# Attention scores in a hybrid decoder block: the lo rows of the queries copied to both partition halves

## The chip, the cores and the metric

The kernel runs on one core of a Trainium2 chip. The metric is the device time of one execution in microseconds, median over the runs. Names of engines: PE is TensorE (PEld its weight loads), DVE is VectorE, ACT is ScalarE, SP is the queue that issues most DMAs; ACT's queue issues some as well.

## The reference, cut to what matters

One layer (DEPTH is 1) over a sequence of 2048 tokens, width 1024, float32. A pre-norm and one combined input projection feed three mixers: a Mamba-2 style SSD with 16 heads, a Conformer convolution with 31 taps, and sliding-window attention with 8 query heads, 2 key-value heads of 64 channels, window 128 and blocks of 128 queries. Their outputs go through one output projection, a post-norm with residual, and a gated per-layer embedding. The attention scores, which the change touches, are

```
s = jnp.einsum('bnqkgd,bnskd->bnkgqs', q, kb).astype(jnp.float32) * (ATTN_HEAD_DIM ** -0.5)
...
s = jnp.where(valid[None, :, None, None], s + bias, -jnp.inf)
m = jnp.maximum(jnp.max(s, axis=-1, keepdims=True), sink)
e = jnp.exp(s - m)
probs = e / (jnp.sum(e, axis=-1, keepdims=True) + jnp.exp(sink - m))
```

For a block of 128 queries `kb` holds 256 keys: the block before and the block itself.

## The kernel before, in words

**Numbers.** Most products run in TensorE's float32r form. Each operand is split into hi (the rounded value) and lo (the rest, exactly), and a product is the sum of hi x lo, lo x hi and hi x hi: three matmuls in `proj` (L443 to L445), `mm3` (L207 to L209) and the output projection (L1042 to L1044).

**Stages.** Phase 1 makes the mixers' outputs and writes them to DRAM; phase 2 is the output projection, phase 3 the gated embedding. Tokens go in four chunks of 512; phase 1 handles them in two halves of two chunks. In each half a list of units is worked through (`C`, `A`, `S`, `G`: convolution, attention, SSD, second B/C group), each for the two chunks p = 0 and p = 1. `A0` to `A3` are the attention units: unit `Aj` does heads j and j + 4, one from each key-value group, in one 128-column projection tile.

**Order.** A unit has a front (a generator that issues projections and evictions and yields every four or eight steps) and a back (softmax and so on), put on the list `pending`. `drive` runs a front; at each yield it advances every pending back by one step and issues some of the waiting convolution taps (L691 on DVE, three per yield in `A` units). The program order so made goes through a scheduler that assigns buffers and orders the instructions of each engine at compile time; on the chip every engine then works its own queue in order.

**Attention.** `attn_front` projects the queries (24 matmuls), evicts them as hi on ACT (`qh`, L708) and lo on DVE (`ql`, L709), copies, and projects the gate (another 24). The keys of a chunk lie ready in two tiles `kT[c][0]` and `kT[c][1]`, one for each key-value group: in partitions 64\*hh to 64\*hh + 63 the hi rows of group hh, in the other 64 partitions its lo rows. So that one matmul over 128 rows gives hi x hi and hi x lo, the hi rows of a query head are needed in both halves: four DMAs on ACT's queue (L713) copy the 64 rows of head hh from `qh` into both halves of `qq[hh]`. The third product, lo x hi, is a second matmul over the 64 rows of `ql` and of the keys where the hi rows lie.

`attn_back` has steps: `scores(0)`, `softmax(0)`; `scores(1)`, `softmax(1)`; `turn(0)`; `mix(0)`, `turn(1)`; `mix(1)`. `scores(u)` fills two PSUM banks (tag `m`, two in all, one for each head) for query blocks 2u and 2u + 1: for each head and block one output of 256 columns, or, for the first block of a chunk, two of 128 columns (the keys before the chunk come from another tile; in the very first block they are left out). DVE (L764) adds the bias, writes the scores to SBUF with their maximum and so frees the banks. ACT takes the exponentials (L790), DVE normalises (L799), PE transposes (L810), ACT copies the transposes out (L817), PE multiplies them with the values (L832).

For p = 0 the steps of the back run between the projections of p = 1; for p = 1 between those of the next unit.

Of the kernel before, what the change touches and what calls it, by code (L numbers as in the profile page):

```python
# [14 lines left out]
P = 128  # L15
# [46 lines left out]
def hybrid_block_kernel(  # L62
# [31 lines left out]
    def t512(name, dtype=F32):  # L94
        return wk.tile([P, TC], dtype, tag="t", name=name, bufs=10)
# [7 lines left out]
    def act_tiles():  # L103
        """(hi, lo) float32r tiles for two 128-channel tiles of one chunk"""
        return act.tile([P, 2, TC], F32R, tag="ah", name="ah"), act.tile([P, 2, TC], F32R, tag="al", name="al")

# [31 lines left out]
    def rsqrt_cols(dst, src, mul, add):  # L138
        """dst = (src * mul + add) ** -0.5 for a few columns, by Newton's iteration."""
        n = src.shape[1]  # L140
        v = wk.tile([P, n], F32, tag="rs_v", name="rs_v", bufs=2)
        V.tensor_scalar(out=v, in0=src, scalar1=mul, scalar2=add, op0=ALU.mult, op1=ALU.add)
        gi = wk.tile([P, n], I32, tag="rs_i", name="rs_i", bufs=2)
        V.tensor_scalar(out=gi, in0=v.bitcast(I32), scalar1=1, scalar2=None, op0=ALU.arith_shift_right)
        g = wk.tile([P, n], F32, tag="rs_g", name="rs_g", bufs=2)
        V.tensor_scalar(out=g.bitcast(I32), in0=gi, scalar1=-1.0, scalar2=float(0x5F3759DF), op0=ALU.mult, op1=ALU.add)
        t = wk.tile([P, n], F32, tag="rs_t", name="rs_t", bufs=2)
        for it in range(3):
            V.tensor_tensor(out=t, in0=g, in1=g, op=ALU.mult)
            V.scalar_tensor_tensor(out=t, in0=t, scalar=-0.5, in1=v, op0=ALU.mult, op1=ALU.mult)  # L150
            V.scalar_tensor_tensor(out=(dst if it == 2 else g), in0=t, scalar=1.5, in1=g, op0=ALU.add, op1=ALU.mult)

    def col_sums(*ts):
        """PSUM [P, n * NB]: sums over the partitions of each t [P, TC], tokens on partitions"""
        pst = ps("m")
        for i, t in enumerate(ts):
            for b in range(NB):
                o_ = 2 * (i * NB + b)
                PE.matmul(pst[:, o_:o_ + 2], lhsT=t[:, b * P:(b + 1) * P], rhs=ones[:, 0:2], start=True, stop=True)
        return pst[:, 0:2 * NB * len(ts)].rearrange("p (b two) -> p b two", two=2)[:, :, 0]  # L160
# [4 lines left out]
    def rstd_cols(ssum, mul, add):  # L165
        """(sums over partitions * mul + add) ** -0.5, tokens on partitions"""
        r = cols()
        rsqrt_cols(r, col_sums(ssum), mul, add)
        return r

    def make_row(r):
        """the column values of r [P, n * NB] as n rows of TC tokens in DRAM"""
        n = r.shape[1]
        pt = ps("m")
        PE.transpose(pt[0:n, 0:P], r, ident)
        rt = wk.tile([n, P], F32, tag="rt", name="rt", bufs=2)
        A.copy(rt, pt[0:n, 0:P])
        row = dram.tile([n // NB, TC], F32, tag=f"row{n}", name="row", bufs=12 if n == NB else NCHUNK)
        nc.scalar.dma_start(out=row.rearrange("i (b t) -> (i b) t", t=P), in_=rt)
        return [row[i, :] for i in range(n // NB)]  # L180

    def load_row(row, rb_=None):
        """[P, TC] tile with a row on every partition"""
        if rb_ is None:
            rb_ = t512("rb_")
        nc.sync.dma_start(out=rb_, in_=row.partition_broadcast(P))
        return rb_
# [5 lines left out]
    def load_w(src, nk=KD):  # L193
        """src [P, nk, P] -> (hi, lo) float32r tiles with hi + lo == src exactly."""
        st = wp.tile([P, KD, P], F32, tag="wst", name="wst", bufs=2)
        nc.sync.dma_start(out=st[:, 0:nk, :], in_=src)
        hi = wp.tile([P, KD, P], F32R, tag="whi", name="whi", bufs=5)
        lo = wp.tile([P, KD, P], F32R, tag="wlo", name="wlo", bufs=5)
        split(hi[:, 0:nk, :], lo[:, 0:nk, :], st[:, 0:nk, :])
        return hi, lo  # L200

    def mm3(out, w, acts, nk, start=True, stop=True):
        """out += sum_k w[:, k].T @ act_k, each as hi*hi + hi*lo + lo*hi."""
        hi, lo = w
        for k in range(nk):
            ah, al = acts(k)
            PE.matmul(out, lhsT=hi[:, k, :], rhs=al, start=start and k == 0, stop=False)  # L207
            PE.matmul(out, lhsT=lo[:, k, :], rhs=ah, start=False, stop=False)  # L208
            PE.matmul(out, lhsT=hi[:, k, :], rhs=ah, start=False, stop=stop and k == nk - 1)  # L209

    # Work is emitted as a stream of projection steps; the mixers' own stages of earlier
    # pieces are slotted between the steps.
# [7 lines left out]
    def sumsq(tiles):  # L220
        """sum of squares of pair tiles over all their channel tiles"""
# [19 lines left out]
    def put(dst, i, src, late=False):  # L241
        """operands i and i + 1 of a chunk from a pair tile"""
# [10 lines left out]
    def stats(c):  # L253
        """rows of the norms that precede the output projection"""
# [30 lines left out]
    def prep(c, ys):  # L285
        """operands of the output projection for chunk c, in the order in which it takes them"""
# [56 lines left out]
    # =====================================================================  # L343
    # Phase 1: pre-norm, input projection and the three mixers
    # =====================================================================
    with ExitStack() as c1:
# [38 lines left out]
        # The first chunk is projected from the weighted input, the projections being scaled by  # L385
        # the norm afterwards, until its norm is there.
        def add_weighed(c, x_, i):
            """operands from two channel tiles scaled by the pre-norm weight alone"""
# [36 lines left out]
        def pre_apply(c):  # L425
            """normalised operands of chunk c"""
# [10 lines left out]
        def proj(ws, c):  # L437
            """project chunk c with each weight tile of ws; yields between steps, returns PSUM tiles"""
# [14 lines left out]
        def dt_tile():  # L453
            """(hi, hi beside lo) of the step-size columns: their two products share a pass"""
# [25 lines left out]
        def ssd_conv(pj, ci, rs_=None):  # L480
            """causal 4-tap convolution and SiLU of one 128-channel tile."""
# [13 lines left out]
        def silu2(pj, name):  # L495
            """2 * silu of a projection in PSUM."""
# [207 lines left out]

        def attn_front(j, p, c, bias, wq, wg):
# [4 lines left out]
            qq = [t512("qq", F32R), t512("qq", F32R)]  # L710
            for hh in range(2):
                for o_ in range(2):
                    nc.scalar.dma_start(out=qq[hh][64 * o_:64 * o_ + 64, :].bitcast(F32), in_=qh[64 * hh:64 * hh + 64, :].bitcast(F32))  # L713
# [3 lines left out]
            pending.append(attn_back(j, c, bias, qq, ql, g2))  # L717
            yield

        def prev(c, i):  # L720
            """the last block of the chunk before c: keys of the two groups, or values"""
# [11 lines left out]
        def attn_back(j, c, bias, qq, ql, g2):  # L733
# [8 lines left out]
            def scores(u):  # L742
# [3 lines left out]
                for hh in range(2):  # L746
                    for bb in range(2):
                        b = 2 * u + bb
                        r = slice(64 * hh, 64 * hh + 64)
# [8 lines left out]
                        for out, kk in parts:  # L758
                            PE.matmul(out, lhsT=qq[hh][:, qs], rhs=kk, start=True, stop=False)  # L759
                            PE.matmul(out, lhsT=ql[r, qs], rhs=kk[r, :], start=False, stop=True)  # L760
# [110 lines left out]
        def ssd_back(q, p, c, Ab, xv, z2, tiles, tabs):  # L871
# [19 lines left out]
            # decayed C and decay matrices  # L891
# [8 lines left out]
            # chunk states  # L900
# [115 lines left out]
    # =====================================================================  # L1016
    # Phase 2: output projection, post-norm and residual
    # =====================================================================
    with ExitStack() as c2:
# [4 lines left out]
        for c in range(NCHUNK):  # L1024
# [3 lines left out]
            # two column pairs side by side at first: the later operands may come later  # L1028
# [39 lines left out]
        # =================================================================  # L1068
        # Phase 3: gated per-layer embedding
        # =================================================================  # L1070
# [22 lines left out]
def _bucket_onehot(np):  # L1093
    """Row b of the result marks the offsets of bucket b, the last row those out of the window."""
# [104 lines left out]
```

## Time and profile before

| what | value |
|---|---|
| runs | 1899.07, 1901.77, 1907.16 us, median 1901.77 |
| profiled execution | span 1898.5 us from first to last instruction, 25052 instructions; 0.6 us below the fastest run |
| mean granted TensorE clock | 0.991 |
| PE busy | 1865.7 us, 98% |
| DVE busy | 1388.0 us, 73% |
| ACT busy | 821.3 us, 43% |
| first and last score matmul | 131.1 and 1241.1 us after the span's start |
| copies of the queries | 64 DMAs of 128 KB on ACT's queue |

How to read it: a row of the timeline has start, duration, engine, line, operation, output <- inputs and shape. Matmuls are pipelined and their ends are modelled, so what a matmul costs in a stream is the distance from its start to the next one's start. The views of waits tell which engine stood idle before an instruction and what ended that.

### The profile page before, as it was taken

How to read it: one execution, taken by the hardware profiler on the slowest of the kernel's cores; microseconds unless marked ns; L12 is line 12 of the kernel's file. 1: busy time of each engine (PE TensorE's matmuls, PEld its weight loads, DVE VectorE, ACT ScalarE, POOL GpSimd, SP SyncE). 2: the span in 40 equal slices, each digit the busy share in tenths (PEclk: the TensorE clock that was granted, in tenths of full speed). 3: DMA queues.
4: the chain of work that ended last, by engine and by line, in shares of the span. 5: the costliest groups of instructions: out<-in, count | busy, mean ns of one | idle time of the engine just before them, and what ended most of it. 6: DMA issues, size and time to landing. Idle time of an engine off the chain costs nothing.

```text
span 1898.5 us, 25052 instructions
## 1 busy us (share of the span) xinstructions
PE 1865.7 (98%) x9386; PEld 1484.6 (78%) x9386; DVE 1388.0 (73%) x2400; ACT 821.3 (43%) x1565; POOL 0.2 (0%) x4
## 2 busy tenths in 40 slices
PE   7999999999999999999999999999999999999999
PEld 5867777787787778778778777777888878887887
DVE  6868678758868875886885886988787767556543
ACT  5435325423825542461553253264553534443332
POOL 0000000000000000000000000000000000000000
PEclk9999999999999999999999999999999999999999
DMA  7432223222532433132232232225677766678553
GB/s 242 123 119 86 67 79 92 65 82 62 161 106 70 133 115 90 43 107 80 78 125 76 57 100 73 83 91 193 234 240 244 235 227 202 209 233 280 187 193 127
DMA packets 113862, 256.69 MB, mean 135 GB/s; under 512 B 11595, under 2 KB 19404, under 8 KB 113740
## 3 DMA queue, kind: packets, MB, share of 16 engines
q1 hardware_dynamic: 108428, 246.65, 40.3%
q10 hardware_dynamic: 5312, 8.44, 1.9%
q8 instruction: 74, 1.21, 0.3%
q14 instruction: 48, 0.39, 0.1%
HBM read 205.05 MB, written 39.50 MB: 129 GB/s over the span
## 4 chain that ended last, share of the span: by engine, by line
PE 80%; DMA 7%; DVE 6%; ACT 4%; issue 2%; SPq 0%; ACTq 0%; DVEq 0%
PE ps_pp L443 15%; PE ps_pp L444 15%; PE ps_pp L445 15%; PE ps_pp L1042 4%; PE ps_pp L1043 4%; PE ps_pp L1044 4%; PE ps_pp L208 3%; PE ps_pp L209 3%; PE ps_pp L207 3%; PE ps_m L760 2%; PE ps_m L759 2%; PE ps_y L934 2%; PE ps_y L832 2%; PE ps_y L931 1%; DMA Ab<-acs_d 1%
## 5 line engine op out<-in xcount | busy, mean ns | idle before, releaser
L443 PE MATMUL ps_pp<-al,whi 128*128 128x512 f32 x1344 | 539.3, 402 | 11.9 <-DVE al L393 9.7
L445 PE MATMUL ps_pp<-ah,whi 128*128 128x512 f32 x1344 | 536.7, 399 | 0.0
L444 PE MATMUL ps_pp<-ah,wlo 128*128 128x512 f32 x1344 | 536.5, 399 | 0.0
L191 DVE TENSOR_TENSOR wlo<-wst,whi 128x1024 fp32r<-128x1024 f32 x214 | 234.2, 1101 | 172.0 <-ACT whi L190 171.4
L443 PEld LDWEIGHTS ps_pp<-al,whi 128*128 128x128 f32 x1344 | 254.9, 190 | 74.0 <-issue 10.1
L190 ACT CAST whi<-wst 128x1024 fp32r<-128x1024 f32 x214 | 203.0, 951 | 251.4 <-PE ps_pp L445 70.8
L691 DVE SCALAR_TENSOR_TENSOR acc<-gl,par_sb,acc 128x1024 f32<-128x1024 f32 x240 | 307.3, 1281 | 2.4
L445 PEld LDWEIGHTS ps_pp<-ah,whi 128*128 128x128 f32 x1344 | 254.9, 190 | 58.4 <-issue 7.3
L444 PEld LDWEIGHTS ps_pp<-ah,wlo 128*128 128x128 f32 x1344 | 255.0, 190 | 56.9 <-issue 5.0
L489 DVE SCALAR_TENSOR_TENSOR cv<-raw,par_sb,cv 128x512 f32<-128x512 f32 x144 | 107.5, 747 | 24.1 <-ACT cv L487 23.4
L208 PE MATMUL ps_pp<-ah,wlo 128*128 128x512 f32 x256 | 100.8, 394 | 4.1 <-DVE wlo L191 4.1
L1042 PE MATMUL ps_pp<-bl,whi 128*128 128x512 f32 x256 | 101.4, 398 | 0.6 <-ACT whi L190 0.6
L1042 PE MATMUL ps_pp<-al,whi 128*128 128x512 f32 x256 | 100.5, 393 | 0.8 <-DVE al L191 0.8
L1043 PE MATMUL ps_pp<-bh,wlo 128*128 128x512 f32 x256 | 100.9, 394 | 0.0
L207 PE MATMUL ps_pp<-al,whi 128*128 128x512 f32 x256 | 100.4, 392 | 0.3 <-ACT whi L190 0.3
L1044 PE MATMUL ps_pp<-bh,whi 128*128 128x512 f32 x256 | 100.7, 394 | 0.0
L209 PE MATMUL ps_pp<-ah,whi 128*128 128x512 f32 x256 | 100.3, 392 | 0.0
L1043 PE MATMUL ps_pp<-ah,wlo 128*128 128x512 f32 x256 | 100.0, 391 | 0.1
L1044 PE MATMUL ps_pp<-ah,whi 128*128 128x512 f32 x256 | 100.0, 391 | 0.0
L790 ACT ACTIVATE S<-S,nm 128x256 f32<-128x256 f32 (+1 forms) x128 | 62.8, 494 | 58.6 <-DVE nm L776 58.6
L897 ACT ACTIVATE Ab<-Ab,acs 128x128 f32<-128x128 f32 x256 | 82.7, 391 | 0.4
L764 DVE CUSTOM_DVE_ANT_0 S<-ps_m,bias,par_sb 128x256 f32<-128x256 f32 (+1 forms) x128 | 58.9, 467 | 5.4 <-PE ps_m L760 5.4
(235 smaller groups left out, 2624.2 us busy)
## 6 DMA issues: line engine op xcount, KB each, us to landing
wst<-in_w_in_dram SPq DMA_DIRECT2D x88, 512.0 KB, 3.5
wst<-in_w_out_dram SPq DMA_DIRECT2D x64, 512.0 KB, 4.3
Ab<-acs_d SPq DMA_DIRECT2D x64, 256.0 KB, 4.0
ysd<-y_d SPq DMA_DIRECT2D x32, 512.0 KB, 5.9
wst<-in_w_gate_dram SPq DMA_DIRECT2D x32, 512.0 KB, 3.5
gl<-in_xT_dram SPq DMA_DIRECT2D x16, 512.0 KB, 3.7
qq<-qh ACTq DMA_DIRECT2D x64, 128.0 KB, 3.0
y_d<-cv SPq DMA_DIRECT2D x32, 256.0 KB, 3.3
```

Source lines behind the costliest of these rows:

```text
L190: A.copy(hi, src)
L191: V.tensor_tensor(out=lo, in0=src, in1=hi.bitcast(F32), op=ALU.subtract)
L207: PE.matmul(out, lhsT=hi[:, k, :], rhs=al, start=start and k == 0, stop=False)
L208: PE.matmul(out, lhsT=lo[:, k, :], rhs=ah, start=False, stop=False)
L209: PE.matmul(out, lhsT=hi[:, k, :], rhs=ah, start=False, stop=stop and k == nk - 1)
L443: PE.matmul(o_, lhsT=hi[:, k, :], rhs=al, start=k == 0, stop=False)
L444: PE.matmul(o_, lhsT=lo[:, k, :], rhs=ah, start=False, stop=False)
L445: PE.matmul(o_, lhsT=hi[:, k, :], rhs=ah, start=False, stop=k == KD - 1)
L691: V.scalar_tensor_tensor(out=acc, in0=gl[:, k:k + 2 * TC], scalar=pc("ccw", j * 31 + k), in1=acc, op0=ALU.mult, op1=ALU.add)
L1042: PE.matmul(pj[dd], lhsT=hi[:, i, :], rhs=yl, start=first, stop=False)
L1043: PE.matmul(pj[dd], lhsT=lo[:, i, :], rhs=yh, start=False, stop=False)
L1044: PE.matmul(pj[dd], lhsT=hi[:, i, :], rhs=yh, start=False, stop=last)
```

## The change

Beside `qh` the lo rows are copied to both partition halves as well. Both go to tiles of one shape, [128 partitions, 2 heads, 512 tokens], from a new ring of three buffers (tag `qd`); `qh` and `ql` stay in the common ring of ten 512-column tiles. Eight DMAs in place of four are issued on ACT's queue in each attention unit. Both score matmuls then take all 128 rows of the key tile: the second one computes lo x hi and lo x lo, where it computed lo x hi before. The number of matmuls stays.

```
+        def qpair(name):
+            return tp.tile([P, 2, TC], F32R, tag="qd", name=name, bufs=3)
+
         def attn_front(j, p, c, bias, wq, wg):
...
-            qq = [t512("qq", F32R), t512("qq", F32R)]
-            for hh in range(2):
-                for o_ in range(2):
-                    nc.scalar.dma_start(out=qq[hh][64 * o_:64 * o_ + 64, :].bitcast(F32), in_=qh[64 * hh:64 * hh + 64, :].bitcast(F32))
+            qq = [qpair("qh2"), qpair("ql2")]
+            for o_ in range(2):
+                r = slice(64 * o_, 64 * o_ + 64)
+                for t, src in zip(qq, (qh, ql)):
+                    for hh in range(2):
+                        nc.scalar.dma_start(out=t[r, hh, :].bitcast(F32), in_=src[64 * hh:64 * hh + 64, :].bitcast(F32))
...
-            pending.append(attn_back(j, c, bias, qq, ql, g2))
+            pending.append(attn_back(j, c, bias, qq, g2))
...
-                        r = slice(64 * hh, 64 * hh + 64)
...
-                            PE.matmul(out, lhsT=qq[hh][:, qs], rhs=kk, start=True, stop=False)
-                            PE.matmul(out, lhsT=ql[r, qs], rhs=kk[r, :], start=False, stop=True)
+                            for i, t in enumerate(qq):
+                                PE.matmul(out, lhsT=t[:, hh, qs], rhs=kk, start=i == 0, stop=i == 1)
...
-    nc = _bacc.Bacc("TRN2", target_bir_lowering=False, num_devices=1)
+    nc = _bacc.Bacc("TRN2", target_bir_lowering=False, num_devices=1, dynamic_dma_scratch_size=1024)
```

The last line makes a reserved scratch area in SBUF smaller, which leaves room for the new ring; the kernel issues no DMA from GpSimd. The rest of the diff takes out comments and docstrings, by which line numbers move.

More of the change, by code (lines that the diff above doesn't have):

```diff
@@ L731, in keep_tail, with attn_back @@
                 kv_tail.append(t)
-        def attn_back(j, c, bias, qq, ql, g2):
+        def attn_back(j, c, bias, qq, g2):
             S, mx, den, nm = {}, {}, {}, {}
```

## The prediction

> **What bounds the kernel now.** I read the page first, its busy shares and its chain of waits.
>
> ```profile
> PE 1865.7 (98%) x9386; PEld 1484.6 (78%) x9386; DVE 1388.0 (73%) x2400; ACT 821.3 (43%) x1565; POOL 0.2 (0%) x4
> ...
> PE 80%; DMA 7%; DVE 6%; ACT 4%; issue 2%; SPq 0%; ACTq 0%; DVEq 0%
> ```
>
> TensorE (PE) is busy all the time and the chain runs through it for 80%. A microsecond taken out of PE's stream is therefore a microsecond of the kernel, as long as PE does not then wait for somebody else. How much the score matmuls take is not to be read from their durations, whose ends are modelled and overlap, but from the distance of starts. So next the timeline of PE and of its weight loads (PEld) around one block of score matmuls, first PE, then PEld (start us, duration us).
>
> ```profile
> 131.08 0.22 PE L759 MATMUL ps_m<-K,qq 128*128 128x128 f32 x1
> ...
> 133.25 0.50 PE L443 MATMUL ps_pp<-al,whi 128*128 128x512 f32 x1
> 133.58 0.40 PE L444 MATMUL ps_pp<-ah,wlo 128*128 128x512 f32 x1
> ...
> 135.65 0.39 PE L444 MATMUL ps_pp<-ah,wlo 128*128 128x512 f32 x1
> 135.87 0.39 PE L445 MATMUL ps_pp<-ah,whi 128*128 128x512 f32 x1
> 136.10 0.28 PE L759 MATMUL ps_m<-K,qq 128*128 128x256 f32 x1
> 136.31 0.38 PE L760 MATMUL ps_m<-K,ql 64*128 64x256 f32 x1
> 136.62 0.38 PE L759 MATMUL ps_m<-K,qq 128*128 128x256 f32 x1
> 136.93 0.38 PE L760 MATMUL ps_m<-K,ql 64*128 64x256 f32 x1
> 137.24 0.50 PE L443 MATMUL ps_pp<-al,whi 128*128 128x512 f32 x1
> 137.58 0.39 PE L444 MATMUL ps_pp<-ah,wlo 128*128 128x512 f32 x1
> ```
>
> ```profile
> 135.88 0.19 PEld L759 LDWEIGHTS ps_m<-K,qq 128*128 128x128 f32 x1
> 136.31 0.18 PEld L760 LDWEIGHTS ps_m<-K,ql 64*128 64x128 f32 x1 [0.24 <-issue]
> 136.62 0.19 PEld L759 LDWEIGHTS ps_m<-K,qq 128*128 128x128 f32 x1
> 136.93 0.18 PEld L760 LDWEIGHTS ps_m<-K,ql 64*128 64x128 f32 x1
> 137.24 0.19 PEld L443 LDWEIGHTS ps_pp<-al,whi 128*128 128x128 f32 x1
> 137.35 0.19 PEld L444 LDWEIGHTS ps_pp<-ah,wlo 128*128 128x128 f32 x1
> 137.58 0.19 PEld L445 LDWEIGHTS ps_pp<-ah,whi 128*128 128x128 f32 x1
> ```
>
> A projection matmul of 512 columns starts 0.225 us after the one before it (135.65 to 136.10 is two). Its weights are loaded while that one runs: the load for L445 starts at 137.58 with the matmul of L444. The score matmuls have half the columns or fewer and yet take 0.31 us each, and each weight load starts at the same moment as its own matmul, so load and product stand one behind the other. It is so wherever an instruction of 64 rows (64\*128) and one of 128 rows follow each other, in both directions, and for the first projection after the block too (137.24 to 137.58, 0.34 in place of 0.225). The first score matmul of the block, behind a 128-row one, had its weights ahead of time (135.88).
>
> **What the change removes.** The count comes from the view of the two source lines (minimum/median/maximum ns):
>
> ```profile
> L759 PE MATMUL ps_m<-K,qq x144: 221/328/581, 131.1 to 1240.8; 128*128 128x256 f32 x96, 128*128 128x128 f32 x48
> ...
> L759 PE MATMUL ps_m<-tail,qq x8: 327/327/474, 759.4 to 1203.0; 128*128 128x128 f32 x8
> ```
>
> L760 has as many: 192 matmuls of 256 columns and 112 of 128. Price before, with the late projection behind each block counted in: 136.10 to 137.58 less a plain 0.225 is 1.255 for four of 256 columns, 0.314 each. The block at 131.08 has four of each kind: 133.58 - 131.08 - 0.225 - 1.255 = 1.02, so 0.255 for one of 128 columns. Together 192 x 0.314 + 112 x 0.255 = 60.3 + 28.6 = 88.9 us.
>
> Price after, when all have 128 rows: no such matmul is in the trace, so bounds. The nearest short ones with 128 rows throughout are these eight (their loads):
>
> ```profile
> 188.44 0.97 PEld L904 LDWEIGHTS ps_m<-xw,Bn 128*128 128x128 f32 x8 [0.17 <-issue]
> ```
>
> Eight starts lie within 0.97 less one load of 0.19, so 0.111 us apart, and I take that as the pace of weight loads, which holds for 128 columns. For 256 columns the floor is the same 0.111 and the ceiling the 0.225 of 512 columns; half of 0.225 is 0.113, just above the load, so I take 0.12, as the two seldom fit perfectly. After: 192 x 0.12 + 112 x 0.111 = 23.0 + 12.4 = 35.4 us. **PE's stream loses 88.9 - 35.4 = 53.5 us** (bounds 55 and 33). The products are as many as before; that the lo rows now meet the lo keys too costs nothing, since rows do not lengthen a matmul (L759 and L760 are 0.31 apart alike).
>
> **What it adds.** Four more copies per unit, 64 more in all, on ScalarE's (ACT's) queue, all before the first score matmul:
>
> ```profile
> 123.17 0.60 ACT L708 ACTIVATE qh<-ps_pp 128x512 fp32r<-128x512 f32 x1 [3.96 <-issue]
> 123.80 2.45 ACTq L713 DMA_DIRECT2D qq<-qh  x4
> ...
> L713 ACTq DMA_DIRECT2D qq<-qh x64: 468/607/1127, 123.8 to 1211.3; - x64
> ...
> DMA to landing us min/median/max: 2.2/3.0/4.9
> ...
> qq<-qh ACTq DMA_DIRECT2D x64, 128.0 KB, 3.0
> ```
>
> Four issues take 2.45 us, 0.61 each. In the first chunk of a pair the scores come at 131.08, 7.9 us after the query eviction starts at 123.17. The eighth copy would be issued at 123.80 + 7 x 0.61 = 128.1 and land 3.0 later, at 131.1: the cover is just used up. I take 0.1 us of PE wait for each of the eight head pairs, 1 us in all; bounds 0 and, with the longest landing of 4.9, 2.0 x 8 = 16 us. The copies of the lo rows wait for DVE's L709, which ends before the third issue.
>
> In the second chunk the copies and the scores stand thus:
>
> ```profile
> 136.93 0.47 ACTq L713 DMA_DIRECT2D qq<-qh  x1
> 139.07 0.40 ACT L790 ACTIVATE S<-S,nm 128x128 f32<-128x128 f32 x1 [1.24 <-DVE nm L776]
> ...
> 139.76 0.47 ACTq L713 DMA_DIRECT2D qq<-qh  x1
> ...
> 158.27 0.33 PE L759 MATMUL ps_m<-K,qq 128*128 128x128 f32 x1
> ```
>
> There the fourth "qd" tile (three buffers) must wait for the last score matmul on the first; queued behind that wait on ACT are the exponentials of L790 and the casts of L190, for which DVE's normalisation and PE's transposes wait. The copies themselves are in no hurry there (its scores come at 158.27), and already now they are spread between the exponentials (136.93, then 139.76 on), so I take 0; ceiling 3 us for each of eight, 24 us. The bytes (64 x 128 KB, 8.4 MB more) go to DMA engines busy for 0.14 of this stretch (next fence): nothing.
>
> **What is late next.** PE is quicker by 53.5 / 8 = 6.7 us in each of eight attention stretches. VectorE (DVE) works there on the convolution taps and the softmax. The windows of 50 us from a first score matmul on (columns: us, PE, PEld, DVE, ACT, POOL busy, granted clock, DMA share, GB/s), and DVE's waits in 130 to 180:
>
> ```profile
> 129.67:179.67 50.00, 49.99 (x245) 37.38 (x245) 43.51 (x94) 20.43 (x59) 0.00 (x0) 1.00 0.14 42
> ...
> sum 400.00, PE 399.74 PEld 299.17 DVE 343.72 ACT 158.87 POOL 0.00; mean PE 49.97 PEld 37.40 DVE 42.97 ACT 19.86 POOL 0.00
> ```
>
> ```profile
> DVE cv L492 <- ACT cth L491: 2.1, 1, 2.1
> DVE rd L792 <- ACT S L790: 1.7, 1, 1.7
> DVE z L499 <- ACT z L498: 1.3, 1, 1.3
> ```
>
> DVE is busy for 43.0 of 50 us; without 6.7 the stretch would last 43.3, and DVE would have to be busy for 99% of it. Its own waits are mostly for ACT evictions that stand behind PE, so they shrink as PE gets quicker, but not all. PE needs DVE there twice per chunk: L764 frees the two score banks, L799 finishes what PE transposes. I take 1.3 us per stretch as waits of PE on DVE, 10 us in all: floor 0, when DVE's taps slide into the stretches between; ceiling half the gain, 27 us.
>
> **The sum.** 53.5 - 1 - 10 = 42.5 us less. The span of the profiled execution, 1898.5, becomes 1856.0. The median of the runs, 1901.77, is 3.3 above that span (the fastest run 0.6): I predict 1859 us, about 2.3% less. Likeliest case alone: 1845 to 1870.
>
> **The rivals.**
>
> *DVE becomes the bound.* The attention stretches shrink by only half, 27 us: 1901.8 - 27 = 1875. For it: the 99% above. Against: the view of PE's waits has no entry at all between 130 and 180 us, and DVE has room in the stretches between.
>
> *Same rows, no overlap.* The Trainium skill, "TensorE: Matmul & The Clock Gate", Part 3, has a rule that speaks against the change: weight loads overlap running matmuls only when the row group differs. It is contradicted by L445's load at 137.58 above. As a mechanism here: 128-row score matmuls would pay load and stream one after the other, 0.111 + 0.113 = 0.224 and 0.111 + 0.056 = 0.167, or 43.0 + 18.7 = 61.7 us, a gain of 27 before the same losses of 6: about 1880.
>
> *The change does not do what it says:* the 0.31 us belongs to the short moving side and not to the rows; then nothing is gained and the copies cost a little: 1903. Against it: the eight of L904 at 0.111.
>
> *Slower: the copies arrive late.* PE stands before the first score matmul of a head pair until the eighth copy is there. With the longest issue (1.127) and landing (4.9): 0.6 + 7 x 1.127 + 4.9 = 13.4 us after the eviction starts, 5.5 past the cover; with ACT held 3 us for the ring in the second chunk it is 8.5 x 8 = 68 us against 53.5 gained: 1901.8 + 14.5 = 1916. It decides from 6.7 us per pair on. For it: there is no cover left. Against: it needs the longest of everything each time.
>
> **How the numbers follow.** Forecast 0.66; DVE bound 0.20; no overlap 0.05; does nothing 0.05; slower 0.04. A measurement of this kernel can tell about 0.5% from no change, 9.5 us. The first three are faster by more than that (0.91), the fourth is the same, the fifth slower. The range holds the forecast and DVE's case up to 1882; its low end, 1844, is the fastest run, 1899.07, less the whole 55 us with no loss.
>
> **What would show it.** Score matmuls of 256 columns 0.11 to 0.13 us apart, of 128 columns 0.11, loads starting ahead of their matmuls, and the projection behind a block 0.225 long. PE's list of waits: some 10 us for DVE (L764, L799) in the attention stretches, about 1 us for the query copies. DVE's busy share near 0.95 there. I am wrong if the starts stay above 0.2 apart (the rows were not the cause), or if they shrink and PE waits more than 20 us for copies or DVE.

## The result, and the profile after

| | median us | runs |
|---|---|---|
| before | 1904.47 | 4, 1899.07 to 1912.59 |
| changed | 1847.54 | 4, 1840.68 to 1850.51 |

The ratio is 0.9701, with a 95% interval of 0.9673 to 0.9729: 3.0% faster, 57 us by the medians. The profiled execution of the changed kernel took 1850.51 us with a span of 1848.7, 49.8 less than the 1898.5 of before. Predicted were 1859 us, in a range of 1844 to 1882. Of all executions below, one, of the kernel with the lo copies on SP's queue, took 2989 us at a mean granted clock of 0.556 and is left out of its median.

The page of the changed kernel, its shares and its chain:

```profile
PE 1810.7 (98%) x9386; PEld 1461.6 (79%) x9386; DVE 1385.1 (75%) x2400; ACT 818.6 (44%) x1565; POOL 0.2 (0%) x4
...
PE 78%; DMA 8%; DVE 6%; ACT 4%; issue 2%; ACTq 1%; SPq 0%; DVEq 0%
```

PE executes as many instructions as before, is still busy 98% of the time and still carries the chain. What shrank is the distance between starts. The timeline of PE, and below it of the weight loads, at the same places as those shown of before (the two score matmuls are now both line 766):

```profile
139.13 0.32 PE L766 MATMUL ps_m<-K,qh 128*128 128x256 f32 x1
139.29 0.28 PE L766 MATMUL ps_m<-K,ql 128*128 128x256 f32 x1
139.41 0.28 PE L766 MATMUL ps_m<-K,qh 128*128 128x256 f32 x1
139.53 0.29 PE L766 MATMUL ps_m<-K,ql 128*128 128x256 f32 x1
139.65 0.40 PE L443 MATMUL ps_pp<-al,whi 128*128 128x512 f32 x1
139.89 0.40 PE L444 MATMUL ps_pp<-ah,wlo 128*128 128x512 f32 x1
```

```profile
135.44 0.19 PEld L766 LDWEIGHTS ps_m<-K,ql 128*128 128x128 f32 x1
135.55 0.19 PEld L766 LDWEIGHTS ps_m<-K,qh 128*128 128x128 f32 x1
...
139.17 0.19 PEld L766 LDWEIGHTS ps_m<-K,ql 128*128 128x128 f32 x1
139.29 0.19 PEld L766 LDWEIGHTS ps_m<-K,qh 128*128 128x128 f32 x1
139.41 0.19 PEld L766 LDWEIGHTS ps_m<-K,ql 128*128 128x128 f32 x1
139.53 0.19 PEld L443 LDWEIGHTS ps_pp<-al,whi 128*128 128x128 f32 x1
```

Matmuls of 256 columns start 0.12 us apart where it was 0.31 (the first of a block up to 0.16); four of them take 0.52 (139.13 to 139.65) where it was 1.14. Each weight load now starts before its own matmul, with the matmul before that (139.29 for the product at 139.41). The projection behind the block has its weights ahead of time again (139.65 to 139.89, 0.24 in place of 0.34). Between matmuls of 128 columns the loads follow each other at 0.11 (135.44 to 135.55), as the prediction read it from L904. From the first start of each block to the start of the projection or other matmul behind it, summed over all 48 blocks of the trace, the 304 score matmuls take 39.7 us where they took 85.9, and the projections behind them some 0.11 x 48 = 5 us less: 51 us in all.

The eight attention stretches, as windows of 43.3 us from the first score matmul of each head pair (columns as in the prediction; first row, the row with the most DVE, and the sum):

```profile
135.44:178.74 43.30, 43.28 (x244) 34.45 (x242) 42.77 (x93) 21.18 (x63) 0.00 (x0) 1.00 0.25 70
...
738.27:781.57 43.30, 42.84 (x249) 34.78 (x248) 43.23 (x93) 21.58 (x63) 0.00 (x0) 1.00 0.26 70
...
sum 346.40, PE 344.95 PEld 277.76 DVE 342.99 ACT 173.11 POOL 0.00; mean PE 43.12 PEld 34.72 DVE 42.87 ACT 21.64 POOL 0.00
```

DVE is busy for 42.87 of 43.3 us, 99%, and yet PE is busy for 43.12. What PE and its loads wait for at the score matmuls, from the view of line 766:

```profile
  issue: 5.1, 22
  DVE mx L770: 2.5, 8
  DMA ql<-ql: 1.8, 4
  PE ps_m L766: 0.5, 1
```

That is 2.5 us for DVE to free the score banks and 1.8 for copies of the lo rows. The view of the transposes (L816), PE's other link to DVE, has no wait for DVE.

### The profile page after: what moved, and what is told of

It is laid out like the page before. It is cut to its first block, busy times and chain, and to the rows that moved or that the text cites. A ratio compares the mean times of both kernels' runs of the same rounds, so it can differ in the third digit from the quotient of the medians.

```text
span 1848.7 us, 25168 instructions
## 1 busy us (share of the span) xinstructions
PE 1810.7 (98%) x9386; PEld 1461.6 (79%) x9386; DVE 1385.1 (75%) x2400; ACT 818.6 (44%) x1565; POOL 0.2 (0%) x4
## 4 chain that ended last, share of the span: by engine, by line
PE 78%; DMA 8%; DVE 6%; ACT 4%; issue 2%; ACTq 1%; SPq 0%; DVEq 0%
PE ps_pp L443 15%; PE ps_pp L444 14%; PE ps_pp L445 14%; PE ps_pp L1048 4%; PE ps_pp L1049 4%; PE ps_pp L1050 4%; PE ps_pp L208 3%; PE ps_pp L209 3%; PE ps_pp L207 3%; PE ps_m L766 2%; PE ps_y L940 2%; PE ps_y L838 2%; DMA Ab<-acs_d 2%; PE ps_y L937 2%; PE ps_m L816 1%
## 5 line engine op out<-in xcount | busy, mean ns | idle before, releaser
L191 DVE TENSOR_TENSOR wlo<-wst,whi 128x1024 fp32r<-128x1024 f32 x214 | 234.1, 1102 | 179.8 <-ACT whi L190 179.4
L796 ACT ACTIVATE S<-S,nm 128x256 f32<-128x256 f32 (+1 forms) x128 | 62.8, 492 | 80.0 <-DVE nm L782 74.6
L937 PE MATMUL ps_y<-Ab,xd 128*64 128x128 f32 x512 | 61.5, 282 | 2.0 <-issue 2.0
```

What stands on the lines that cost most here:

```text
L191: V.tensor_tensor(out=lo, in0=src, in1=hi.bitcast(F32), op=ALU.subtract)
```

## The experiments

**Copies without the 128 rows.** All of the change but one line is kept:

```
-    PE.matmul(out, lhsT=t[:, hh, qs], rhs=kk, start=i == 0, stop=i == 1)
+    r = slice(64 * hh, 64 * hh + 64) if i else slice(0, P)
+    PE.matmul(out, lhsT=t[r, hh, qs], rhs=kk[r, :], start=i == 0, stop=i == 1)
```

> The eight copies, the new tiles and the ring of three stay as in the changed kernel; only the second score matmul goes back to the 64 rows of its head. Theory (the border between 64 and 128 rows costs the overlap of weight load and product): the starts go back to 0.31 us for 256 columns and 0.255 for 128, the 304 score matmuls take about 86 us again, and the kernel is at 1898 to 1910 us, the time of before or up to 5 us more for the copies. Rival (what was gained came from the other edits, the tiles that leave the common ring earlier or the smaller scratch): it stays near 1848 us.

Measured: 1904.6 us, ratio to before 1.0021 (0.9995 to 1.0047), as the theory had it. The starts are back at the old distance, in its timeline (line 767):

```profile
140.56 0.38 PE L767 MATMUL ps_m<-K,ql 64*128 64x256 f32 x1
140.87 0.39 PE L767 MATMUL ps_m<-K,qh 128*128 128x256 f32 x1
141.19 0.38 PE L767 MATMUL ps_m<-K,ql 64*128 64x256 f32 x1
141.50 0.50 PE L444 MATMUL ps_pp<-ah,wlo 128*128 128x512 f32 x1
```

Between this kernel and the changed one lies nothing but the rows of the second matmul, and with them the whole gain. The new ring, the smaller scratch and the earlier release of the query tiles give nothing by themselves, and 64 more copies cost nothing that can be measured.

**Half the borders.** The kernel before, with hi and lo turned round in every second pair:

```
+    flips = 0
...
-    PE.matmul(out, lhsT=qq[hh][:, qs], rhs=kk, start=True, stop=False)
-    PE.matmul(out, lhsT=ql[r, qs], rhs=kk[r, :], start=False, stop=True)
+    two = [(qq[hh][:, qs], kk), (ql[r, qs], kk[r, :])]
+    for i, (w, x) in enumerate(two if flips % 2 == 0 else two[::-1]):
+        PE.matmul(out, lhsT=w, rhs=x, start=i == 0, stop=i == 1)
+    flips += 1
```

> The kernel before, with the order of hi and lo turned round in every second pair: hi lo, lo hi, hi lo, lo hi. The count of matmuls and copies is that of before; borders between 64 and 128 rows fall from 304 to about 150, and two lo matmuls with 64 rows follow each other. Theory 1 (each border costs, two 64-row matmuls of one row group overlap like two of 128): lo after lo starts 0.11 to 0.12 us after it, half of the 53 us is gained, about 1875 us. Theory 2 (a 64-row matmul never overlaps its weight load with anything): lo after lo stays at 0.31 and 0.255; only hi after hi is cheap, 76 times some 0.17 us, about 1889 us. Rival (rows are no cause): 1902 us.

Measured: 1867.1 us, ratio 0.9818 (0.9777 to 0.9860). A block of four in its timeline, the two lo matmuls of 64 rows in one row of x2, and below it their weight loads:

```profile
136.77 0.28 PE L762 MATMUL ps_m<-K,qq 128*128 128x256 f32 x1
136.98 0.50 PE L762 MATMUL ps_m<-K,ql 64*128 64x256 f32 x2
137.41 0.38 PE L762 MATMUL ps_m<-K,qq 128*128 128x256 f32 x1
137.63 0.39 PE L443 MATMUL ps_pp<-al,whi 128*128 128x512 f32 x1
137.86 0.40 PE L444 MATMUL ps_pp<-ah,wlo 128*128 128x512 f32 x1
```

```profile
136.98 0.29 PEld L762 LDWEIGHTS ps_m<-K,ql 64*128 64x128 f32 x2 [0.24 <-issue]
```

The block takes 0.86 us, and the projection behind it its plain 0.23. With the projection's surplus the block of before took 1.14 + 0.11 = 1.25 with four borders between 64 and 128 rows, here it is 0.86 with two, in the changed kernel 0.52 with none: steps of 0.39 and 0.34, some 0.18 us for a border. So it is the border that costs, and not the 64 rows: theory 2 would have kept the lo matmuls at 0.31 each. Between the two lo matmuls the load runs ahead, as theory 1 has it: two loads lie within 0.29 us, one takes 0.18, so they start 0.11 apart. The sign that theory 1 named, starts of the matmuls 0.11 to 0.12 apart, is not in the trace: they start 0.22 apart, since the row of the first lo matmul begins together with its own load and holds that load's 0.11 as well.

Over all blocks the 304 score matmuls take 62.8 us, and with the projections behind them 28 us less than before, close to the 27 expected. The measured 35 us hold some 7 more, the size of what the clock below gives (median 0.9945 against 0.991 of the kernel before beside it, 0.0035 of 1900 us).

The same trace shows one thing more. Where the lo matmuls of the two heads follow each other, they use different halves of the rows, and the two stand in one row:

```profile
159.20 0.38 PE L762 MATMUL ps_m<-K,ql 64*128 64x256 f32 x2
159.51 0.44 PE L762 MATMUL ps_m<-K,qq 128*128 128x128 f32 x2
```

One of 256 and one of 128 columns take 0.38 us together, as long as the first alone; in all 11 such places they start 2 to 4 ns apart. The two halves work side by side. No version here was built on that.

**What the copies cost.** The changed kernel with only the hi copies; the second score matmul reads them again:

```
-            qq = [qpair("qh2"), qpair("ql2")]
+            qq = [qpair("qh2")]
...
-                            for i, t in enumerate(qq):
+                            for i, t in enumerate((qq[0], qq[0])):
```

> The changed kernel without the copies of the lo rows: the second score matmul reads the hi copies again, so the lo part of the queries is left out of the scores. Its score matmuls all have 128 rows; ACT issues four DMAs per unit as before, and the ring of three is never short. It prices the copies. Theory: they cost the waits of PE for the landing of the eighth copy and little else, 1 to 3 us, so 1843 to 1849 us. Rival (ACT held by the ring and the issues delays exponentials and with them PE): 10 us or more are gained, under 1840 us.

Measured: 1849.3 us, ratio 0.9716 (0.9678 to 0.9755), as the changed kernel (0.9701). The copies of the lo rows are hidden, to what can be measured. In the traces the 304 score matmuls take 37.5 us without them and 39.7 with them, so the waits for them are some 2 us.

**Less and more DVE work in the attention stretches.** Taps per step from 3 to 2, and to 4:

```
-        TAPS = {"A": 3, "C": 1, "S": 2, "G": 1}
+        TAPS = {"A": 2, "C": 1, "S": 2, "G": 1}
```

> The changed kernel with two convolution taps per step in the attention units in place of three; the taps left over are done in the following units. Theory (PE waits for DVE in the attention stretches, some 4 of the 10 us that were forecast): these waits shrink, 1 to 4 us are gained, 1843 to 1847 us. Rival (DVE has room, or the taps now press on the SSD units): no change or some us more, 1848 to 1856 us.

> The changed kernel with four taps per step in the attention units in place of three: some 8 taps, 10 us of DVE work, move into each pair of attention units. Theory (DVE would be busy for longer there than PE, 53 us against 43): PE waits for DVE, 10 to 30 us more than the changed kernel, 1852 to 1875 us. Rival (DVE has room): the same within 4 us or a little less.

Measured with two taps: 1863.8 us, ratio 0.9790 (0.9742 to 0.9837); with four: 1840.9, ratio 0.9696 (0.9677 to 0.9715). Four taps are as fast as three (0.9682 on the same chip, intervals overlap); two are slower than either expectation had it, so what PE could save of waits for DVE there was small beside what came in place. The run with four taps says nothing on the theory that DVE binds: from the first scores on, the eight windows of 43.3 us hold as many taps as with three (19, in one window 15), and DVE is busy for 42.4 us in place of 42.9. After the scores of the first pair, from 167 to 185 us, no tap runs at all, so there were none left to move in and the 10 us of DVE work never came. With two taps it is 16 of them and 40.8 us. The list of PE's waits with two taps tells what came in place:

```profile
PE ps_m L766 <- DMA ql<-ql: 11.2, 8, 2.0
...
PE ps_m L505 <- DVE cv L492: 7.4, 4, 6.5
```

Fewer taps move the rest of the order: eight times PE now stands before the score matmuls for the copies, for up to 2.0 us. That is the bound that the prediction gave its term for the copies (2.0 us for each of eight, 16 in all), reached in another order of the work.

**The copies on two queues.** With two taps, the lo copies go to SP's queue:

```
-    nc.scalar.dma_start(out=t[r, hh, :]...
+    (nc.scalar if src is qh else nc.sync).dma_start(out=t[r, hh, :]...
```

> The changed kernel with two taps per step in the attention units, and the copies of the lo rows issued on SP's queue in place of ACT's, so that four hi and four lo copies are issued side by side. With two taps alone PE stood 11.2 us for lo copies, up to 2.0 us at a time. Theory (the eighth copy comes too late there because eight issues of 0.6 us stand in one queue): these waits go to under 3 us and the kernel gains 8 to 12 us, 1852 to 1856 us. Rival (the copies are late for the transfers in flight beside them, or two taps cost elsewhere): 1860 us or more.

Measured: 1862.2 us, ratio 0.9797 (0.9758 to 0.9836), no better than two taps alone. Its list of PE's waits has no copy at its head any more:

```profile
PE ps_m L505 <- DVE cv L492: 13.7, 9, 6.0
PE ps_pp L443 <- DVE al L393: 10.0, 1, 10.0
```

The 304 score matmuls fell from 52.5 to 37.8 us in their blocks, which fits the theory that eight issues in one queue make the copies late there; but the time was not gained, as the rival had it. The waits of transposes for DVE's L492, the end of the SSD convolution, grew from 7.4 to 13.7 us, and one of the output projection for L191 from 3.8 to 8.0. So most of the wait that is removed there comes back later. Of the 21 us that still part this kernel from the changed one beside it, some 10 go with the granted clock (0.991 against 0.9965); the rest is not named by these lists.

The same edit with three taps:

> The changed kernel with its three taps, the copies of the lo rows issued on SP's queue, those of the hi rows on ACT's. Theory (the cover of 7.9 us before the first scores is just used up, and PE waits 1 to 2 us for the eighth copy in all): these waits go, 1 to 3 us less than the changed kernel. Rival (lo copies stand in SP's queue behind weight loads that wait for buffers): waits for lo copies grow, 3 us or more above it.

Measured: 1844.1 us, ratio 0.9709 (0.9686 to 0.9732), against 0.9682 (0.9662 to 0.9702) of the changed kernel on the same chip: no gain, perhaps a small loss; the intervals overlap. The theory fails: the 304 score matmuls take 37.6 us in its trace against 39.9 in that of the changed kernel beside it, so the 2 us of waits went, but the time did not follow.

**A ring of four.**

```
-            return tp.tile([P, 2, TC], F32R, tag="qd", name=name, bufs=3)
+            return tp.tile([P, 2, TC], F32R, tag="qd", name=name, bufs=4)
```

> The changed kernel with four buffers in the ring of the copied queries in place of three, so that the lo tile of the second chunk of a pair waits for no score matmul; the scratch goes from 1024 to 512 bytes to make room. Theory (ACT's waits at the ring, some 20 us in its list, lie off PE's path): the same as the changed kernel within 3 us. Rival (they hold the exponentials and so PE): 5 us or more less.

Measured: 1839.7 us, ratio 0.9693 (0.9673 to 0.9712): the same. The wait at the ring is not on PE's path.

**Taps left out.** 24 of the 30 multiply-add taps, with both score forms:

```
-            for k in range(30):
+            for k in range(24, 30):
```

> The changed kernel with 6 of the 30 multiply-add taps of each convolution in place of 30: 24 taps are left out, some 31 us of DVE work per convolution, nearly all of it in the attention stretches. It shows what PE still waits for DVE there. Theory (about 4 to 6 us of such waits are left in the changed kernel): 4 to 8 us less than the changed kernel, 1839 to 1844 us. Rival 1 (DVE took more of the gain than that, as forecast, 10 us or more): under 1837 us. Rival 2 (none): the same within 2 us.

> The kernel before with the same 24 taps left out of each convolution. There PE stood before no attention instruction for DVE, so theory: the same as before within 3 us, 1897 to 1905 us, and the distance to the changed kernel with 6 taps is the full 55 us. Rival (taps cost PE time before as well, so the attention stretches were bound by DVE in part already): 5 us or more below before.

Measured: 1873.3 us, ratio 0.9865 (0.9830 to 0.9899), and 1917.9 us, ratio 1.0099 (1.0062 to 1.0135). No theory had that: with less DVE work both kernels are slower, by 32 and 17 us against their own forms beside them. The order moved: the score matmuls stand in 33 and 35 blocks in place of 48, presumably because the scheduler has less to lay between the steps. In the kernel before with 6 taps PE waits like this:

```profile
PE ps_m L505 <- DVE cv L492: 17.1, 7, 2.8
...
PE ps_m L904 <- DVE xw L890: 6.1, 7, 2.3
PE ps_m L759 <- DMA qq<-qh: 4.6, 4, 2.2
```

As a price of DVE work these two runs are void, since the order moved with the work. Much of the loss goes with the clock: its median is 0.9855 in place of 0.9965 for the changed kernel, 0.980 in place of 0.992 for the one before, 0.011 of 1873 us and 0.012 of 1918 us, some 20 and 23 us. What they do show is that less DVE work alone does not make these kernels faster. The gain of the 128 rows is there in this order as well, 45 us.

**The standards.** The changed kernel beside the second and the third group of runs:

> The changed kernel once more, on the chip of the runs beside it, as their standard: 1840 to 1852 us.

> The changed kernel as the standard of the three beside it: 1838 to 1850 us.

Measured: 1841.0 us, ratio 0.9699 (0.9667 to 0.9731), and 1839.0 us, ratio 0.9682 (0.9662 to 0.9702). None of the other versions is faster than the changed kernel beyond its interval.

## Why the prediction was right, point by point

**The borders.** "PE's stream loses 88.9 - 35.4 = 53.5 us": in the trace it is 85.9 + 5 - 39.7 = 51, with the waits inside the blocks counted in. The mechanism is shown by the copies alone (no gain) and by half the borders (28 of these 51 us), the price of 0.12 and 0.11 by the starts. The rival "the change does not do what it says" falls with it, and "same rows, no overlap" too: the weight loads of 128-row matmuls run ahead, 0.11 apart. By the way it came out, the Trainium skill's "TensorEngine Tiling (Array Packing)", section Key Properties, has the fitting rule: a change of tiling mode drains TensorE, a change of tile alone does not. The runs agree and give it a price, some 0.18 us for each border here, and none where lo matmuls of the two heads meet in different halves. The drain itself is in no trace here.

**The copies.** "The cover is just used up", 1 us: the eighth copy was issued within the last pair of this ACT view,

```profile
127.52 0.60 ACT L711 ACTIVATE qh<-ps_pp 128x512 fp32r<-128x512 f32 x1 [3.95 <-issue]
128.15 1.15 ACTq L720 DMA_DIRECT2D qh<-qh  x2
...
131.94 1.25 ACTq L720 DMA_DIRECT2D ql<-ql  x2
```

and with scores at 135.44 the cover was again 7.9 us. PE and its loads waited 1.8 us for lo copies in all; a copy landed 2.4 us after its issue in the median (4.2 at most), where the sum had taken 3.0. Late copies were real, but in another order of the work (two taps). The 0 for the ring in the second chunk holds: four buffers are no faster than three.

**The step that failed in size** is "I take 1.3 us per stretch as waits of PE on DVE, 10 us in all". It argued that DVE could not be busy for 99% of a stretch without holding PE. It was busy for 99% (42.87 of 43.3, where the prediction named 0.95), and PE waited 2.5 us in place of 10 at the one of its two links to DVE, the score banks, and not at the other, the transposes. DVE's own idle time shrank from 7.0 of 50 us to 0.4 of 43.3, where the prediction had expected that a part of it would stay. So the floor of that term was the nearer end, and the rival "DVE becomes the bound" is not borne out by this kernel. Whether still more DVE work there would hold PE was not tried, since four taps brought none.

**What the sum left out** is the granted clock, below: 0.991 in the profile before, 0.994 after.

From the profiled pair: the 51 of the blocks, in which the waits at the score matmuls are already paid, stand against the 42.5 forecast for the three terms together, and 49.8 were measured in the span. From the first score matmul to the last it is 53.4 us (131.1 to 1241.1 before, 135.4 to 1192.0 after). Ahead of the first, where the change has no part, this execution of the changed kernel was 4.4 us slower (in its later traces the first score matmul is at 130.8 and 131.3); there its clock was 0.96 in place of 0.99, which is some 4 us. In between, the clock was at half for 17.1 us before and 3.4 after, worth some 7 us, a part of them inside the blocks and so counted already; a few us of that are not seen in the 53.4 and are not assigned here. In the later executions, with a higher clock, the distance was 60 us by the medians.

**Luck.** The medians of the changed kernel there, 1841.0 and 1839.0 us, lie below the low end of the range, 1844, which was worked out as the whole 55 us with no loss and nothing for the clock. That the first measurement lies inside, at a clock of 0.993 to 0.997, is in part luck; the mechanism is not.

## What to carry to other kernels

On TensorE look at the distance of starts, and at whether a weight load starts before or together with its own matmul; where matmuls of 64 and 128 rows alternated, each border cost the overlap, some 0.18 us, whatever the products needed. Filling the rows, even with copies that compute something superfluous, takes the borders away; merely ordering the matmuls so that equal row counts follow each other took half of them away and half of the blocks' cost. An engine that is busy for 99% of a stretch is not yet the bound: what counts is how long the bounding engine waits for it. Taking work away from it can cost more by the new order than it saves.

## What had not been expected of the hardware

The granted clock of TensorE falls to half for some microseconds at a time, and the alternation of rows seems to bring that about. In the kernel before, around the second half's last but one attention unit (timeline of PE, then windows of that kernel and of the one with the copies alone; the clock is the number before the DMA share):

```profile
1069.11 0.31 PE L759 MATMUL ps_m<-K,qq 128*128 128x128 f32 x1
...
1070.43 0.42 PE L760 MATMUL ps_m<-K,ql 64*128 64x256 f32 x1
1070.78 0.80 PE L444 MATMUL ps_pp<-ah,wlo 128*128 128x512 f32 x1
1071.38 0.31 PE L759 MATMUL ps_m<-K,qq 128*128 128x128 f32 x1
1071.62 0.47 PE L760 MATMUL ps_m<-K,ql 64*128 64x128 f32 x1
```

```profile
1071.00:1074.40 3.40, 3.40 (x8) 2.21 (x9) 1.38 (x9) 0.00 (x0) 0.00 (x0) 0.50 0.02 5
```

```profile
1107.00:1117.00 10.00, 10.00 (x23) 6.65 (x23) 5.71 (x17) 1.76 (x5) 0.00 (x0) 0.50 0.01 5
```

PE counts as busy all the time in these windows. The first example leaves another reading open: ahead of 1069.11 stand a wait of 0.2 us and eight matmuls of two columns (0.9 us). At 455.75 to 459.03 in the same trace there are twelve score matmuls with a border at each and nothing between them, and the clock is halved from 459.6 on:

```profile
455.75 0.33 PE L759 MATMUL ps_m<-K,qq 128*128 128x128 f32 x1
...
458.72 0.38 PE L760 MATMUL ps_m<-K,ql 64*128 64x256 f32 x1
459.03 0.50 PE L444 MATMUL ps_pp<-ah,wlo 128*128 128x512 f32 x1
459.37 0.40 PE L445 MATMUL ps_pp<-ah,whi 128*128 128x512 f32 x1
459.61 0.58 PE L443 MATMUL ps_pp<-al,whi 128*128 128x512 f32 x1
459.99 0.63 PE L444 MATMUL ps_pp<-ah,wlo 128*128 128x512 f32 x1
```

"TensorE: Matmul & The Clock Gate" of the Trainium skill, Part 1, describes such a gate: the activity of the array is watched in windows of 3.4 us, and too little of it halves the clock. Lengths and ratio agree with these windows; in that reading the array stands idle at the borders. In the changed kernel's profile all eight attention windows have a clock of 1.00. Between the first and the last score matmul of the head pairs the clock was at half for 13.7 us in the trace of before, 30.7 with the copies alone, 3.4 with half the borders, 13.7 with two taps, where PE waited for copies, and never in the seven traces with 128 rows throughout and three or four taps.

The mean clock of the executions: 0.985 to 0.995, median 0.991, in 29 of the kernel before; 0.984 to 0.991, median 0.9875, in 10 with the copies alone; 0.993 to 0.999, median 0.997, in 13 of the changed kernel. 0.006 of 1900 us is 11 us; the measured 57 to 60 us exceed the 51 of the blocks by 6 to 9, which is of that size. That the clock is higher without the row borders is shown by these runs; on one chip the copies alone had at most 0.991, and the kernel with only the hi copies, 128 rows throughout, at least 0.993. That an idle array at the borders is the cause is argued only, and borders are not the only cause: the two-tap kernels, where PE waits for other reasons, have a low clock too (0.989 to 0.992), and the two with six taps one of 0.980 to 0.989.
